# Queueing weight pieces behind the first tile's activation split in a two-layer decoder trunk

## The chip, the core and the metric

The kernel runs on one core of a Trainium2 chip. The metric is the device time of one execution in microseconds (us), launch to end; the median of the runs is what is compared. The engines are named as the profile names them: PE is TensorE, PEld its weight loads, DVE is VectorE, ACT is ScalarE, POOL is GpSimd, SP is the engine that issues the transfers.

## The reference

Two layers over 256 tokens of width 1024, all in float32. Every sub-layer is wrapped in two RMS norms, and the six of them follow one another: FFN, attention with short convolution, FFN, FFN, RWKV-7 mixing, FFN.

```python
def macaron_half_ffn(x, pre_g, post_g, w_gate, w_up, w_down):
    h = rmsnorm(x, pre_g)
    h = (jax.nn.silu(h @ w_gate) * (h @ w_up)) @ w_down
    return x + 0.5 * rmsnorm(h, post_g)

for i in range(DEPTH):
    x = macaron_half_ffn(x, *p["ffn1"])
    x = x + rmsnorm(p["mixer"](rmsnorm(x, pre_g), *p["mix"]), post_g)
    x = macaron_half_ffn(x, *p["ffn2"])
```

## The kernel before

**Tiles and parts.** The 256 tokens are two tiles of 128 rows, m=0 and m=1, kept in x0 and x1. The six sub-layers are six parts, so there are five places where a new part begins after another has ended. This text calls them start 1 (attention, near 190 to 203 us), start 2 (second FFN, near 337 to 352), start 3 (third FFN, near 527 to 541), start 4 (RWKV mixing, near 717 to 745) and start 5 (last FFN, near 954 to 968).

**Products in three passes.** A float32 product is made of three matmuls: each operand is split into a high part `hi`, rounded to the matmul type, and the rest `lo`; mm3 (lines 282 to 284) adds hi·hi, hi·lo and lo·hi. So each weight and each activation has to be split before TensorE can take it. For a weight piece of 128x1024, split_u and split_free issue one ACT copy (L241, `hi`) and then the subtraction (L246, `lo`), on DVE as one instruction, or on POOL as two halves of 128x512. Every `share`-th piece goes to POOL; `nlo` counts them. For activations `split` (L217 on ACT, L218 on DVE) does the same, from PSUM after a transpose.

**The end of a part.** out_proj multiplies with the last weight matrix. In its tail it first finishes tile 0 and then runs tile 1. As soon as tile 0's sums are there, post_norm(0) updates x0 (square sums on ACT at L297, L290; the power for 1/rms on POOL at L291; L353 and L356 on DVE), and `after(0)` calls the next part's start(0): pre_norm (L297, L314, L290, L291, L319), eight transposes (L326) and hT_split. The PE instructions of tile 1 from step PIN=15 on, the last three matmuls, stand behind those transposes. start(1) follows when tile 1 is done.

**What stands beside it.** While PE runs tile 1, the next part's first weights are loaded and split: in an FFN eight pieces for 512 columns, four of the gate matrix and four of the up matrix. This text counts them as piece 1, 2 and so on, in the order in which split_u is called. There are 18 buffers `u`, two a piece, and out_proj's tail holds most of them until tile 1 has used its weights.

**The order.** Instructions are put in order on each engine by a planner that runs a model of the chip while the program is built and takes, among those ready, the one that was written first. `issue_after(i)` adds one rule: an instruction on the engine of `i` comes behind `i`. pre_norm(0) sets `held` to three instructions, the last square sum (ACT), the last product with the gain (DVE, L314) and the power (POOL), and `free` to 4. split_u counts `free` down; the first four pieces are not held, all later ones stand behind `held`, each engine behind its own.

**In the RWKV part** l1_start takes the place of norm_in's start: it calls pre_norm and so sets `held` and `free` too, but transposes and copies by its own lines (L902 to L905). Its first pieces are one of w_r, two of mixed activations (L246 `u<-xn`), and a second one of w_r.

Of the kernel before, what the change touches and what calls it, by code (L numbers as in the profile page):

```python
# [8 lines left out]
F32 = mybir.dt.float32  # L9
F32R = mybir.dt.float32r  # L10
AF = mybir.ActivationFunctionType
ALU = mybir.AluOpType
# [17 lines left out]
class Trunk:  # L30
# [161 lines left out]
    def norm_in(self, gname):  # L192

        hilo = []

        def start(m, first=False):
            if m < 0:
                hilo.extend([(self.gain_cols if first else self.gain)(gname), *self.hl_tiles()])
                return
            g, *hl = hilo  # L200
            if g.shape[1] == KD:
                self.hT_split(self.pre_norm(m), hl, m, g)
            else:
                self.hT_split(self.pre_norm(m, g), hl, m)
        return hilo, start

    def gain(self, name):
# [6 lines left out]


    def split(self, src, hi, lo):
        self.nc.scalar.activation(hi, src, AF.Copy)  # L217
        return self.nc.vector.tensor_sub(lo, src, hi.bitcast(F32))  # L218

    def split_u(self, src):  # L220

# [6 lines left out]
    def split_free(self, src):  # L228
        n = src.shape[1]
        hi, lo = (self.u(F32R)[:, :n * src.shape[2]].rearrange("p (a b) -> p a b", a=n) for _ in range(2))  # L230
        self.nlo += 1
        if n == 1 and src.shape[2] == 512:

            if self.nlo % 3 == 0:
                self.nc.vector.tensor_copy(hi, src)
                self.nc.gpsimd.tensor_sub(lo, src, hi.bitcast(F32))
            else:
                self.split(src, hi, lo)
            return hi, lo
        pool = self.share and self.nlo % self.share == 0  # L240
        self.nc.scalar.activation(hi, src, AF.Copy)  # L241
        ax = 1 if n > 1 else 2
        m = src.shape[ax] // (2 if pool else 1)
        for i in range(0, src.shape[ax], m):
            c = (slice(None),) * ax + (slice(i, i + m),)
            (self.nc.gpsimd if pool else self.nc.vector).tensor_sub(lo[c], src[c], hi[c].bitcast(F32))  # L246
        return hi, lo
# [59 lines left out]
    def pre_norm(self, m, g=None):  # L307
        nc = self.nc
        xn, xg = self.xn(), self.x[m] if g is None else self.xn()
        ss = []  # L310
        for sl in self.HALF:
            self.tail_of["sq"] = self.sum_in(ss, xn[:, sl], self.x[m][:, sl], 1.0 / 32, EPS).ins
            if g is not None:
                self.tail_of["xg"] = nc.vector.tensor_tensor(xg[:, sl], self.x[m][:, sl], g[:, sl], op=ALU.mult).ins  # L314
        r = self.rstd(ss)
        if m == 0 and g is not None:
            self.held, self.free = list(self.tail_of.values()), 4
        for sl in self.HALF:
            nc.vector.tensor_scalar(xn[:, sl], xg[:, sl], r, None, op0=ALU.mult)  # L319
        return xn  # L320

    def transposed(self, src, n):
# [7 lines left out]
    def hT_split(self, xn, t, m, g=None):  # L330
        for h in range(2):
            pt = self.transposed(xn[:, h * 512:(h + 1) * 512], 4)
            hi, lo = (t[h][:, :, i, m * P:(m + 1) * P] for i in range(2))
            if g is None:
                self.split(pt, hi, lo)
                continue
            for i in range(4):
                k = h * 4 + i
                self.nc.scalar.activation(hi[:, i], pt[:, i, :], AF.Copy, scale=g[:, k:k + 1])
                self.nc.vector.scalar_tensor_tensor(lo[:, i], pt[:, i, :], g[:, k:k + 1], hi[:, i].bitcast(F32),  # L340
                                                    op0=ALU.mult, op1=ALU.subtract)

    def post_norm(self, m, g, half):

        nc = self.nc
        c = 0.5 if half else 1.0
        t, sq, ss = self.xn(), self.xn(), []

        def take(b):
            sl = self.HALF[len(ss)]  # L350
            self.sum_in(ss, sq[:, sl], b, 1.0 / (32 * c), EPS / (c * c))
            r = self.rstd(ss) if len(ss) == 2 else None
            nc.vector.tensor_mul(t[:, sl], b, g[:, sl])  # L353
            if r is not None:
                for sl in self.HALF:
                    nc.vector.scalar_tensor_tensor(self.x[m][:, sl], t[:, sl], r, self.x[m][:, sl],  # L356
                                                   op0=ALU.mult, op1=ALU.add)
        return take


    def out_proj(self, w, a, order, split, gname, half, after, by_k=False):
        ws = {}
        gpost = self.gain(gname)
# [14 lines left out]
        for i in range(split):  # L378
            for m in range(2):
                for hh in range(2):  # L380
                    step(i, m, hh)
            yield
        tail = range(split, len(order))
        take = self.post_norm(0, gpost, half)
        steps = [(i, hh) for hh in range(2) for i in tail]
# [1149 lines left out]
```

## Time and profile before

| | us |
|---|---|
| median of 3 runs | 1160.28 (1158.94 to 1164.31) |
| profiled execution | 1160.69 |
| its span in the trace | 1159.0 |
| PE busy in the span | 1093.6 |
| DVE busy | 701.2 |
| ACT busy | 601.0 |
| POOL busy | 429.6 |

The rows come from the one profiled execution. A row of the timeline gives the start in us, the length in us, the engine, the source line, the operation and its tiles, the shapes and a count where like instructions follow one another; in brackets stands the idle time before it and what released it. A row of the window view gives the window, its length, the busy time with the number of instructions, the granted TensorE clock as a share of full speed, and what the transfers did.

### The profile page before, as it was taken

What the parts mean: (1) busy time and instruction counts of PE and PEld (TensorE: products, weight loads), DVE (VectorE), ACT (ScalarE), POOL (GpSimd) and SP (SyncE); (2) the same over time, 40 slices, a digit from 0 to 9 for tenths busy, and PEclk for the clock granted to TensorE, in tenths of its full rate; (3) what the DMA queues carried; (4) which work ended last, traced back from release to release, by engine and by line L of the source; (5) the groups of instructions that cost most, each with busy time, mean ns of one, the idle gap of its engine ahead of it and who ended that gap; (6) DMA issues with size and microseconds to landing.
All of it is one profiled execution on the core that took longest, in us unless ns stands there. A gap on an engine that the chain in (4) does not pass through costs nothing.

```text
span 1159.0 us, 16840 instructions
## 1 busy us (share of the span) xinstructions
PE 1093.6 (94%) x6429; PEld 921.9 (80%) x6429; DVE 701.2 (61%) x1177; ACT 601.0 (52%) x1130; POOL 429.6 (37%) x390
## 2 busy tenths in 40 slices
PE   7999998998989999999999999997789789999997
PEld 5888887997967888887888888786447777888886
DVE  6655526656767655426655543889894797655531
ACT  7655545245645555435655542557554355655541
POOL 3523233232544333333532332334463553433331
PEclk9999999989999999999999999999996899999999
DMA  9765563442445765655566553442212144755530
GB/s 331 252 216 180 184 207 89 148 146 73 163 164 168 231 207 171 205 182 180 164 201 200 184 184 126 145 147 74 92 54 92 57 150 160 244 192 188 176 109 36
DMA packets 130749, 187.46 MB, mean 162 GB/s; under 512 B 6871, under 2 KB 101087, under 8 KB 130670
## 3 DMA queue, kind: packets, MB, share of 16 engines
q1 hardware_dynamic: 130670, 186.41, 48.7%
q8 instruction: 50, 0.82, 0.3%
q14 instruction: 29, 0.24, 0.1%
HBM read 185.34 MB, written 1.05 MB: 161 GB/s over the span
## 4 chain that ended last, share of the span: by engine, by line
PE 76%; DVE 15%; issue 4%; ACT 3%; POOL 1%; DMA 0%; SPq 0%; DVEq 0%; POOLq 0%; ACTq 0%
PE mm L429 10%; PE fl L429 10%; PE fl L284 7%; PE fl L282 6%; PE fl L283 6%; PE fl L430 5%; PE mm L430 5%; PE mm L282 5%; PE mm L284 5%; PE mm L283 5%; DVE u L246 3%; PE tr L326 2%; PE fl L433 1%; PE mm L433 1%; DVE xn L1220 1%
## 5 line engine op out<-in xcount | busy, mean ns | idle before, releaser
L246 POOL TENSOR_TENSOR u<-raw,u 128x512 fp32r<-128x512 f32 x222 | 321.7, 1471 | 496.1 <-ACT u L241 490.4
L241 ACT ACTIVATE u<-raw 128x1024 fp32r<-128x1024 f32 x312 | 327.5, 1058 | 276.7 <-PE mm L283 78.5
L246 DVE TENSOR_TENSOR u<-raw,u 128x1024 fp32r<-128x1024 f32 x201 | 272.7, 1362 | 210.5 <-ACT u L241 210.2
L429 PE MATMUL mm<-b,u 128*128 128x512 f32 x504 | 181.3, 398 | 0.0
L429 PE MATMUL fl<-b,u 128*128 128x512 f32 x504 | 180.6, 397 | 0.0
L430 PE MATMUL fl<-b,u 128*128 128x256 f32 x504 | 141.5, 281 | 0.0
L430 PE MATMUL mm<-b,u 128*128 128x256 f32 x504 | 141.4, 281 | 0.0
L284 PE MATMUL fl<-u,b 128*128 128x512 f32 (+1 forms) x304 | 118.4, 390 | 3.5 <-DVE b L218 3.0
L282 PE MATMUL fl<-u,b 128*128 128x512 f32 (+1 forms) x304 | 118.7, 393 | 2.6 <-DVE u L800 1.3
L283 PE MATMUL fl<-u,b 128*128 128x512 f32 (+1 forms) x304 | 118.4, 389 | 1.5 <-DVE u L246 1.5
L282 PE MATMUL mm<-u,b 128*128 128x512 f32 (+1 forms) x296 | 114.7, 389 | 0.0
L283 PE MATMUL mm<-u,b 128*128 128x512 f32 (+1 forms) x296 | 113.0, 383 | 0.0
L284 PE MATMUL mm<-u,b 128*128 128x512 f32 (+1 forms) x296 | 112.5, 382 | 0.0
L429 PEld LDWEIGHTS mm<-b,u 128*128 128x128 f32 x504 | 94.8, 188 | 19.7
L429 PEld LDWEIGHTS fl<-b,u 128*128 128x128 f32 x504 | 94.9, 188 | 19.5
L430 PEld LDWEIGHTS mm<-b,u 128*128 128x128 f32 x504 | 95.2, 189 | 3.3
L430 PEld LDWEIGHTS fl<-b,u 128*128 128x128 f32 x504 | 95.2, 189 | 3.1
L284 PEld LDWEIGHTS fl<-u,b 128*128 128x128 f32 x304 | 57.8, 190 | 16.9 <-DVE b L218 4.3
L282 PEld LDWEIGHTS fl<-u,b 128*128 128x128 f32 x304 | 58.0, 191 | 15.1 <-ACT b L217 2.0
L283 PEld LDWEIGHTS fl<-u,b 128*128 128x128 f32 x304 | 58.0, 191 | 12.9 <-DVE u L246 1.7
L282 PEld LDWEIGHTS mm<-u,b 128*128 128x128 f32 (+1 forms) x296 | 55.8, 189 | 11.8 <-issue 0.7
L283 PEld LDWEIGHTS mm<-u,b 128*128 128x128 f32 (+1 forms) x296 | 55.9, 190 | 10.6
(313 smaller groups left out, 1830.0 us busy)
## 6 DMA issues: line engine op xcount, KB each, us to landing
raw<-in_l_ffn_w_up_dram SPq DMA_DIRECT2D x44, 1024.0 KB, 7.3
raw<-in_l_ffn_w_down_dram SPq DMA_DIRECT2D x44, 1024.0 KB, 5.1
raw<-in_l_ffn_w_gate_dram SPq DMA_DIRECT2D x42, 1024.0 KB, 5.3
raw<-in_l_w_in_dram SPq DMA_DIRECT2D x9, 1024.0 KB, 5.2
raw<-in_l_w_v_dram SPq DMA_DIRECT2D x6, 1024.0 KB
raw<-in_l_w_out_dram SPq DMA_DIRECT2D x4, 1024.0 KB
raw<-in_l_w_r_dram SPq DMA_DIRECT2D x4, 1024.0 KB, 5.6
raw<-in_l_w_k_dram SPq DMA_DIRECT2D x4, 1024.0 KB, 5.2
```

The costliest lines, as they stand in the source:

```text
L241: self.nc.scalar.activation(hi, src, AF.Copy)
L246: (self.nc.gpsimd if pool else self.nc.vector).tensor_sub(lo[c], src[c], hi[c].bitcast(F32))
L282: mm(out, a[0], b[0], start=start, stop=False)
L283: mm(out, a[0], b[1], start=False, stop=False)
L284: mm(out, a[1], b[0], start=False, stop=stop)
L326: t = self.nc.tensor.transpose(pt[:, j * P:(j + 1) * P], src[:, j * P:(j + 1) * P], self.ident)
L429: mm(b2, w[k][0], x, start=k == 0, stop=False)
L430: mm(b2[:, 0], w[k][1], x[:, 0], start=False, stop=False)
L433: mm(b2, w[k][0], x, start=False, stop=True)
L1220: ins = [e.tensor_tensor(x, x, t, op=ALU.subtract) for e, x, _, _, t in act]
```

## The change

Three edits. pre_norm(0) no longer keeps the product with the gain in `held` but the second half of the scaling by 1/rms (L319), which comes later on DVE. norm_in's start(0), used by the FFN and attention parts, then replaces the first two entries of `held` by the last two instructions of hT_split: the ACT copy and the DVE subtraction of the second half of tile 0's transposed activations; the third entry, POOL's power, stays. And a piece that is free (`free` not yet below 0) is never given to POOL: its `lo` is one DVE instruction, whatever `nlo` says. `split` and hT_split return their instructions for this.

```diff
@@ norm_in
-                self.hT_split(self.pre_norm(m, g), hl, m)
+                hi, lo = self.hT_split(self.pre_norm(m, g), hl, m)
+                if m == 0:
+                    self.held[:2] = hi.ins, lo.ins
@@ split_free
-        pool = self.share and self.nlo % self.share == 0
+        pool = self.share and self.nlo % self.share == 0 and self.free < 0
@@ pre_norm
             if g is not None:
-                self.tail_of["xg"] = nc.vector.tensor_tensor(xg[:, sl], self.x[m][:, sl], g[:, sl], op=ALU.mult).ins
+                nc.vector.tensor_tensor(xg[:, sl], self.x[m][:, sl], g[:, sl], op=ALU.mult)
         r = self.rstd(ss)
+        for sl in self.HALF:
+            self.tail_of["xn"] = nc.vector.tensor_scalar(xn[:, sl], xg[:, sl], r, None, op0=ALU.mult).ins
         if m == 0 and g is not None:
-            self.held, self.free = list(self.tail_of.values()), 4
-        for sl in self.HALF:
-            nc.vector.tensor_scalar(xn[:, sl], xg[:, sl], r, None, op0=ALU.mult)
+            self.held, self.free = [self.tail_of[n] for n in ("sq", "xn", "pow")], 4
```

## Rows read from the trace of the kernel before

**Rows 1.** The page, busy time, share of the span and instructions of each engine.

```profile
PE 1093.6 (94%) x6429; PEld 921.9 (80%) x6429; DVE 701.2 (61%) x1177; ACT 601.0 (52%) x1130; POOL 429.6 (37%) x390
```

**Rows 2.** Timeline of PE at starts 1, 2, 3, 4 and 5.

```profile
198.60 1.09 PE L326 MATMUL tr<-ident,xn 128*128 128x128 f32 x8 [1.78 <-DVE xn L319]
...
202.46 0.50 PE L284 MATMUL fl<-u,b 128*128 128x512 f32 x1 [1.35 <-DVE b L218]
...
346.28 1.33 PE L326 MATMUL tr<-ident,xn 128*128 128x128 f32 x8 [4.06 <-DVE xn L319]
...
351.63 0.50 PE L284 MATMUL fl<-u,b 128*128 128x512 f32 x1 [1.09 <-DVE b L218]
...
536.66 0.66 PE L326 MATMUL tr<-ident,xn 128*128 128x128 f32 x4 [0.93 <-DVE xn L319]
538.07 0.66 PE L326 MATMUL tr<-ident,xn 128*128 128x128 f32 x4 [0.75 <-DVE xn L319]
...
540.90 0.50 PE L284 MATMUL fl<-u,b 128*128 128x512 f32 x1 [0.57 <-DVE b L218]
...
725.70 1.04 PE L326 MATMUL tr<-ident,xn 128*128 128x128 f32 x8
...
962.97 0.63 PE L326 MATMUL tr<-ident,xn 128*128 128x128 f32 x4 [1.29 <-DVE xn L319]
964.43 0.80 PE L326 MATMUL tr<-ident,xn 128*128 128x128 f32 x4 [0.84 <-DVE sse L300]
```

**Rows 3.** Windows of PE: busy time, count, granted clock, DMA share, GB/s.

```profile
346.00:351.00 5.00, 4.26 (x15) 0.66 0.20 49
...
535.00:538.00 3.00, 1.39 (x8) 1.00 0.42 110
...
541.00:551.00 10.00, 10.00 (x44) 1.00 0.93 314
...
965.00:968.00 3.00, 3.00 (x9) 0.50 0.49 134
```

**Rows 4.** Timeline of ACT at starts 1, 2 and 3.

```profile
193.29 0.30 ACT L290 ACTIVATE rstd<-ss,sse 128x1 f32<-128x1 f32 x1 [0.75 <-DVE sse L300]
...
336.99 0.28 ACT L290 ACTIVATE rstd<-ss,sse 128x1 f32<-128x1 f32 x1
...
344.03 2.93 ACT L241 ACTIVATE u<-raw 128x1024 fp32r<-128x1024 f32 x3
...
531.17 0.28 ACT L290 ACTIVATE rstd<-ss,sse 128x1 f32<-128x1 f32 x1
```

**Rows 5.** Timeline of POOL at starts 1, 2 and 3.

```profile
192.62 3.91 POOL L246 TENSOR_TENSOR u<-raw,u 128x512 fp32r<-128x512 f32 x2 [0.63 <-ACT u L241]
...
337.17 2.52 POOL L246 TENSOR_TENSOR u<-raw,u 128x512 fp32r<-128x512 f32 x2 [6.59 <-ACT u L241]
339.65 0.56 POOL L291 TENSOR_TENSOR rstd<-rstd,nhalf 128x1 f32<-128x1 f32 x1
...
531.34 4.24 POOL L246 TENSOR_TENSOR u<-raw,u 128x512 fp32r<-128x512 f32 x2 [4.13 <-ACT u L241]
```

**Rows 6.** Timeline of DVE at start 2, and one row of start 5.

```profile
340.25 1.41 DVE L356 SCALAR_TENSOR_TENSOR x<-xn,rstd,x 128x512 f32<-128x512 f32 x2 [3.38 <-POOL rstd L291]
341.58 1.29 DVE L314 TENSOR_TENSOR xn<-x,gain 128x512 f32<-128x512 f32 x2
...
345.65 0.88 DVE L319 TENSOR_SCALAR xn<-xn,rstd 128x512 f32<-128x512 f32 x2 [0.45 <-POOL rstd L291]
346.45 4.53 DVE L246 TENSOR_TENSOR u<-raw,u 128x1024 fp32r<-128x1024 f32 x2
350.90 1.27 DVE L218 TENSOR_TENSOR b<-tr,b 128x512 fp32r<-128x512 f32 x2
...
957.17 2.38 DVE L314 TENSOR_TENSOR xn<-x,gain 128x512 f32<-128x512 f32 x2
```

**Rows 7.** Line 246 on DVE: length of one in ns, shortest, median, longest; span of starts.

```profile
L246 DVE TENSOR_TENSOR u<-raw,u x201: 1207/1225/2358, 21.5 to 1126.5; 128x1024 fp32r<-128x1024 f32 x101
```

More of the change, by code (lines that the diff above doesn't have):

```diff
@@ L216, in split @@
     def split(self, src, hi, lo):
-        self.nc.scalar.activation(hi, src, AF.Copy)
-        return self.nc.vector.tensor_sub(lo, src, hi.bitcast(F32))
+        i = self.nc.scalar.activation(hi, src, AF.Copy)
+        return i, self.nc.vector.tensor_sub(lo, src, hi.bitcast(F32))
     def split_u(self, src):
@@ L334, in hT_split @@
             if g is None:
-                self.split(pt, hi, lo)
+                last = self.split(pt, hi, lo)
                 continue
@@ L341, in hT_split @@
                                                     op0=ALU.mult, op1=ALU.subtract)
+        return last if g is None else None
     def post_norm(self, m, g, half):
```

## The prediction

> **What bounds the kernel now.** The page's first part comes first: PE is busy 94% of the span, DVE and ACT little over half of it [rows 1]. A gain must therefore come out of the 65 us in which PE stands still, or out of stretches in which its clock is low. So the second view is PE's timeline, read only for rows with a bracket, in the stretches where one part ends and the next begins. At four of the five starts PE stands twice [rows 2]: before the transposes of tile 0 (released by L319 on DVE, the scaling by 1/rms, or by L300, a small DVE step behind it), and before the first L284, the first matmul that needs the `lo` of the transposed activations (released by L218 on DVE). Start 1 loses 1.78 + 1.35 = 3.13 us, start 2 4.06 + 1.09 = 5.15, start 3 0.93 + 0.75 + 0.57 = 2.25, start 5 1.29 + 0.84 = 2.13: 12.66 us together. Start 4 shows no bracket, so nothing can be won there on PE at once.
>
> The third view is the windows with the granted clock [rows 3]. Behind the stand of 4.06 us PE runs at 0.66 on average over 5 us, and behind the two stands of start 5 at 0.50, the lower level of 1.2 GHz, for 3 us; behind start 3's stands it keeps 1.00. At full clock a matmul of 512 columns follows the last after 10.00 us / 44 = 0.227 us. At start 5 nine are counted in the 3 us, where full speed needs some 2.0; with the slow transposes ahead of them I put the loss at 1.5 to 1.9 us. At start 2 15 instructions stand in the slow window; seven matmuls at double distance cost 7 x 0.227 = 1.6 us. The most that can be had is then 12.66 + 1.6 + 1.9 = 16.2 us.
>
> Last, ACT, POOL and DVE are read backwards from each stand to see what was late. At start 3 ACT has the sum ready at 531.17 + 0.28 = 531.45 [rows 4], but POOL is 4.24 us in a weight piece from 531.34 to 535.58 [rows 5], and the power, for which L319 waits, comes behind it. At start 1 the sum is ready at 193.59 and POOL is in a piece until 196.53; at start 2 at 337.27, and the power begins at 339.65 behind a piece of 2.52 us [rows 4, 5]. These are pieces 4, 4 and 4 of the new part: free ones, which the old hold lets by. Then at start 2 two pieces take DVE 4.53 us, from 346.45, directly ahead of L218 at 350.90 [rows 6]: held pieces, but held only behind L314.
>
> **Part one: free pieces leave POOL.** By the counting of `nlo`, and by the POOL rows at each start, nine pieces move: pieces 2 and 4 at start 1, 1 and 4 at starts 2, 3 and 4, piece 3 at start 5. Removed: 18 POOL halves, 1.26 us each undisturbed [rows 5]; added: nine DVE instructions at 1.21 to 2.36 us, median 1.23 [rows 7]. I take the median, since the long ones are those beside POOL work, which is what goes. Powers no longer wait: 196.53 - 193.59 = 2.9 us at start 1, about 2.3 at start 2, 4.1 at start 3, none at start 5. At start 5 the gain is on DVE: both L314 take 2.38 us beside a POOL piece and 1.29 where POOL is idle [rows 6], and the L356 pair ahead of them is lengthened alike, so some 2 us. What it costs: at most two pieces a start on DVE, 1.23 each, ready before the power is; POOL's wait was longer than the piece. At start 2 piece 4 can be ready at 337.1 and L356 at 337.9, so it pushes L356 by 0.4 at most.
>
> That a lengthening of DVE comes with POOL at work is what the two L314 rows show. The Trainium skill (SBUF — State Buffer, Who interferes with whom) says that a DVE instruction with two SBUF inputs and a GpSimd one that reads SBUF exclude each other for a whole instruction; by that rule, an estimate, nine pieces of two halves would give DVE back up to 18 x 1.26 = 23 us, of which only what lies on the chains above counts. The trace agrees in direction: 2.38 against 1.29 us.
>
> **Part two: the hold moves.** Pieces 5 and on now stand behind the second ACT copy and the second DVE subtraction of tile 0's split. Removed from in front of them: at start 2 4.53 us of DVE, and ACT's piece ahead of the second sum; at starts 3 and 5 one or two pieces each between the two halves of L218. At start 1 piece 5 stands there. What waits instead: each piece 5 to 8, its buffers, the transfers of the next raw weights that SP issues when a raw tile is done, and the up matmuls. Cover: behind the first L284 the gate product of tile 0 alone is 24 matmuls, 24 x 0.227 = 5.4 us, and four pieces cost ACT 2.93 / 3 = 0.98 each [rows 4], DVE 1.23 [rows 7], POOL 2.5 to 4.2 for its one [rows 5]. The second L218 ends 1.27 / 2 = 0.6 us behind the first [rows 6], so the first up piece is there 0.6 + 0.98 + 1.23 = 2.8 us after the first L284, POOL's, if it is the third, at 0.6 + 3 x 0.98 + 4.2 = 7.7 at worst, and the up product needs them at 5.4, 6.8, 8.2 and 9.5. So I cost the delay at nothing; without that cover it costs about 2.5 us a start. SP's transfers come as early as before: the pieces begin later relative to the norm, but the norm ends sooner.
>
> **Chain of start 2 with both edits.** Power at 337.3, L356 at 337.9 to 338.3 (1.41 us for the pair), L314 1.29 us, sum and power 1.0 to 1.2 us, L319 at 342.0: transposes at 342.5 or so. PE is free at 346.28 - 4.06 = 342.2. So of 4.06 about 0.3 to 0.8 stays; L218 no longer has the two pieces in front, which takes the 1.09; a stand under 1 us, like start 3's, leaves the clock at 1.00. I take 5.2 of at most 6.8. **Start 1:** the power is early enough that L319 is done before PE is free at 196.8, so 1.78 goes; of the 1.35 some stays, since splits by `split` (not held) also stand in front of L218: 2.3 of 3.13. **Start 3:** 2.0 of 2.25. **Start 5:** DVE's 2 us cover the first stand, 1.29, and with it I take half of the clock's 1.9; the second, 0.84, I leave, since piece 3 may take 1.2 of DVE: 2.2 of 4.0. **Start 4:** two more pieces on DVE, between -2.4 (both hidden, POOL's share of DVE time freed) and +2.5 (two medians in line); the first is split while DVE is idle and the second replaces a POOL piece, so 0. Sum: 5.2 + 2.3 + 2.0 + 2.2 = 11.7 us. Bounds: 16.2 + 2.4 = 18.6 at best; with the half of each start and +2.5 at start 4, 3.4 at worst of this case.
>
> **The rivals.** *A, only the POOL edit tells.* If what the planner put between the halves stays (free pieces and unheld splits fill the same places), the second stands remain: 1.8 + 2.3 + 1.0 + 1.3 = 6.4 us gained. For it: start 1 has unheld work; against: start 2's two pieces are held ones. *B, the up weights become the wait.* If DVE and ACT take tile 1's norm first (L356, L314, L319: 1.41 + 1.29 + 0.88 = 3.6 us [rows 6]), pieces 5 to 8 come 2.5 to 3.6 us later and PE waits that long at starts 2, 3 and 5, 7.5 to 10.8 us: net 0.9 to 4.2 gained, against it the 5.4 us of cover. *C, slower: DVE becomes the engine at the starts.* Its place is from L356 to L218. If all nine pieces stand in line there, they cost 9 x 1.23 to 9 x 2.36 = 11 to 21 us against the 6.4 that POOL's power gives: 5 to 15 us slower, 1170 in the middle. It decides where DVE's norm work (3.6 us) and its pieces exceed PE's remaining tile-1 matmuls: at start 2 those end 4.3 us after L356 can begin (337.9 to 342.2), so one piece tells there; at starts 1 and 3 the sum for L319's power is ready 3.2 and 4.3 us ahead of their end (193.59 to 196.82, 531.45 to 535.73), room for two. The Trainium skill (Perfetto Trace Analysis, Optimizing Scalar/DVE Operations) holds that offloading to GPSIMD may make sense where DVE is saturated, which speaks against taking pieces off POOL; DVE at 61% of the span [rows 1] and idle 3.38 us ahead of L356 [rows 6] shows that it isn't, here. *D, the change doesn't do what it says:* at start 4 it doesn't (no split in the hold); elsewhere the planner's model could already place the pieces late, and the time stays within 2 us of 1160.
>
> **How the numbers follow.** The profiled execution took 1160.69 us, 0.4 over the median of the runs: 1160.69 - 11.7 = 1149.0, which I give without taking off the 0.4. Chances: forecast (gain 8 to 18) 0.66; A 1154.3, 0.14; B 1156.5 to 1160, 0.08; C 0.06; D 0.06. Range: 1143.5 (nearly all of the bound) to 1156.5 (A with a loss at start 4). Differences under 0.5%, 5.8 us, can hardly be told from none. Faster by more: the forecast and most of A, 0.77; within: 0.17; slower: 0.06.
>
> **What would show it.** Right: POOL 390 - 18 = 372 instructions and DVE 1177 + 9 = 1186; no POOL L246 between the two powers of a start; no L246 on DVE between L319 and the second L218 unless of pieces 1 to 4; brackets before L326 of under 1 us at each start; a clock of 1.00 behind start 2. Wrong: PE brackets on `u` L246 or L241 some 5 us behind the first L284 (B), or L319 released by DVE's own queue rather than by POOL, with L246 in front (C). What would upset all of it: the planner orders anew, and the attention and RWKV parts between may come out differently by a few us either way.

## The result, and the profile after

The changed kernel took 1151.08 us (median of 4 runs, 1149.36 to 1152.56) against 1162.3 for the kernel before; the ratio is 0.9884, 95% interval 0.9843 to 0.9925. Two later measurements of the same program gave 0.992 (0.988 to 0.996) and 0.9895 (0.9863 to 0.9928). One execution of the third run below, of 1346.6 us at a granted clock of 0.75, is left out of its ratio. The profiled execution took 1152.56 us with a span of 1150.8, 8.2 under the span before. In the changed file the lines have moved by two or three: L328 are the transposes, L284 to L286 the three matmuls, L219 and L220 the activation split, L243 and L248 the weight pieces, L292 and L293 the sum and the power, L359 the update of x, L316 the product with the gain; L319 is still the scaling. In the runs below the numbers move by a few more; the operation and its tiles tell which step a row is.

The page's first part shows the pieces moved: POOL has 18 instructions fewer, DVE 9 more [rows 1].

```profile
PE 1092.3 (95%) x6429; PEld 918.5 (80%) x6429; DVE 701.9 (61%) x1186; ACT 600.1 (52%) x1130; POOL 406.9 (35%) x372
```

PE's timeline at the five starts: the transposes of tile 0, the first matmul that needs the `lo` of its activations, and the transposes of tile 1.

```profile
196.75 1.03 PE L328 MATMUL tr<-ident,xn 128*128 128x128 f32 x8
199.90 0.50 PE L286 MATMUL fl<-u,b 128*128 128x512 f32 x1 [0.71 <-DVE b L220]
208.89 1.07 PE L328 MATMUL tr<-ident,xn 128*128 128x128 f32 x8 [0.89 <-DVE xn L319]
...
338.56 1.06 PE L328 MATMUL tr<-ident,xn 128*128 128x128 f32 x8 [0.17 <-DVE xn L319]
340.62 0.47 PE L286 MATMUL fl<-u,b 128*128 128x512 f32 x1
352.78 1.06 PE L328 MATMUL tr<-ident,xn 128*128 128x128 f32 x8 [1.39 <-DVE xn L319]
...
526.64 1.03 PE L328 MATMUL tr<-ident,xn 128*128 128x128 f32 x8
528.67 0.47 PE L286 MATMUL fl<-u,b 128*128 128x512 f32 x1
540.84 1.07 PE L328 MATMUL tr<-ident,xn 128*128 128x128 f32 x8 [1.40 <-DVE xn L319]
...
952.65 1.06 PE L328 MATMUL tr<-ident,xn 128*128 128x128 f32 x8 [0.18 <-DVE xn L319]
954.71 0.48 PE L286 MATMUL fl<-u,b 128*128 128x512 f32 x1
968.69 1.29 PE L328 MATMUL tr<-ident,xn 128*128 128x128 f32 x8 [3.26 <-DVE xn L319]
```

In the kernel before no bracket stood before tile 1's transposes. Starts 2 and 5:

```profile
361.73 1.04 PE L326 MATMUL tr<-ident,xn 128*128 128x128 f32 x8
...
978.12 1.03 PE L326 MATMUL tr<-ident,xn 128*128 128x128 f32 x8
```

At tile 0 little is left of the stands of [rows 2]: 0.71, 0.17, nothing and 0.18 us. But four new ones stand before tile 1's transposes: 0.89, 1.39, 1.40 and 3.26. Set side by side, the same points of both traces tell what each was worth; "PE free" is the start of the transposes less the bracket.

| point | before | after | earlier by |
|---|---|---|---|
| start 1, PE free for tile 0 | 196.82 | 196.75 | 0.1 |
| first matmul with `lo` | 202.46 | 199.90 | 2.6 |
| first matmul behind tile 1's transposes | 211.75 | 210.58 | 1.2 |
| start 2, PE free | 342.22 | 338.39 | 3.8 |
| first with `lo` | 351.63 | 340.62 | 11.0 |
| behind tile 1 | 363.01 | 354.09 | 8.9 |
| start 3, PE free | 535.73 | 526.64 | 9.1 |
| first with `lo` | 540.90 | 528.67 | 12.2 |
| behind tile 1 | 552.29 | 542.15 | 10.1 |
| start 4, transposes | 725.70 | 717.17 | 8.5 |
| start 5, PE free | 961.68 | 952.47 | 9.2 |
| first with `lo` | 968.01 | 954.71 | 13.3 |
| behind tile 1 | 979.40 | 970.01 | 9.4 |
| end | 1159.0 | 1150.8 | 8.2 |

From "PE free" to the first matmul with `lo`, tile 0 gains 2.5 + 7.2 + 3.1 + 4.1 = 16.9 us; from there to the point behind tile 1's transposes 1.4 + 2.1 + 2.1 + 3.9 = 9.5 us are given back. At starts 2, 3 and 5 both sums hold some work that only changed sides: before, seven matmuls ran between the transposes and the first with `lo`, after, five. Two matmuls at 0.227 us are 0.45 a start, some 1.4 us in all. Without them tile 0 gains 2.5 + 6.7 + 2.7 + 3.6 = 15.5 us and tile 1 loses 1.4 + 1.6 + 1.6 + 3.5 = 8.1, of which 6.9 are its four stands. Behind two of the stands, at starts 3 and 5, a further 1.6 and 1.2 go to the clock, as the windows behind starts 2, 3 and 5 show:

```profile
352.00:357.00 5.00, 3.98 (x23) 1.00 0.80 288
541.00:546.00 5.00, 4.75 (x20) 0.67 0.61 223
968.00:973.00 5.00, 4.28 (x17) 0.66 0.05 15
```

The attention part between starts 1 and 2 gave another 2.7 us, of which more in the last section. Within it PE now waits twice for a weight piece, some 30 and 36 us behind start 1's tile 1; before, only 0.18 us stood in that stretch:

```profile
240.78 0.39 PE L286 MATMUL fl<-b,u 128*128 128x256 f32 x1 [0.73 <-DVE u L248]
...
246.78 0.38 PE L285 MATMUL mm<-u,b 64*128 64x256 f32 x1 [0.94 <-DVE u L220]
```

Why is tile 1 late? DVE and POOL at start 2, from the split of tile 0 to the scaling of tile 1:

```profile
339.85 1.29 DVE L220 TENSOR_TENSOR b<-tr,b 128x512 fp32r<-128x512 f32 x2 [1.05 <-ACT b L219]
341.28 1.23 DVE L248 TENSOR_TENSOR u<-raw,u 128x1024 fp32r<-128x1024 f32 x1
...
343.03 1.22 DVE L248 TENSOR_TENSOR u<-raw,u 128x1024 fp32r<-128x1024 f32 x1
344.69 3.48 DVE L359 SCALAR_TENSOR_TENSOR x<-xn,rstd,x 128x512 f32<-128x512 f32 x2 [0.44 <-POOL rstd L293]
...
348.69 1.21 DVE L248 TENSOR_TENSOR u<-raw,u 128x1024 fp32r<-128x1024 f32 x1
...
350.49 1.21 DVE L248 TENSOR_TENSOR u<-raw,u 128x1024 fp32r<-128x1024 f32 x1
352.14 0.88 DVE L319 TENSOR_SCALAR xn<-xn,rstd 128x512 f32<-128x512 f32 x2 [0.44 <-POOL rstd L293]
```

```profile
343.04 1.62 POOL L293 TENSOR_TENSOR rstd<-rstd,nhalf 128x1 f32<-128x1 f32 x1 [5.15 <-ACT rstd L292]
344.62 2.99 POOL L248 TENSOR_TENSOR u<-raw,u 128x512 fp32r<-128x512 f32 x2
351.09 1.02 POOL L293 TENSOR_TENSOR rstd<-rstd,nhalf 128x1 f32<-128x1 f32 x1 [3.48 <-ACT rstd L292]
```

The hold does what it says: no piece stands ahead of L220. But pieces 5 to 9 have not gone away. They now stand beside the norm of tile 1: DVE's pieces between its steps, and POOL's piece 7 over the update of x, which takes 3.48 us for the pair where it took 1.41 [rows 6]. At start 5 POOL costs twice. ACT has the sum ready at 957.05, POOL has just begun piece 6, and the power waits until 960.46; the update then meets POOL's next piece:

```profile
956.75 0.30 ACT L292 ACTIVATE rstd<-ss,sse 128x1 f32<-128x1 f32 x1
```

```profile
956.95 3.55 POOL L248 TENSOR_TENSOR u<-raw,u 128x512 fp32r<-128x512 f32 x2 [4.97 <-ACT u L243]
960.46 1.53 POOL L293 TENSOR_TENSOR rstd<-rstd,nhalf 128x1 f32<-128x1 f32 x1
961.96 2.98 POOL L248 TENSOR_TENSOR u<-raw,u 128x512 fp32r<-128x512 f32 x2
```

```profile
962.02 3.47 DVE L359 SCALAR_TENSOR_TENSOR x<-xn,rstd,x 128x512 f32<-128x512 f32 x2 [0.44 <-POOL rstd L293]
```

### The profile page after: what moved, and what is told of

It reads as the page before. It is cut to its first block, busy times and chain, and to the rows that moved or that the text cites. A ratio compares the mean times of both kernels' runs of the same rounds, so it can differ in the third digit from the quotient of the medians.

```text
span 1150.8 us, 16819 instructions
## 1 busy us (share of the span) xinstructions
PE 1092.3 (95%) x6429; PEld 918.5 (80%) x6429; DVE 701.9 (61%) x1186; ACT 600.1 (52%) x1130; POOL 406.9 (35%) x372
## 4 chain that ended last, share of the span: by engine, by line
PE 73%; DVE 13%; issue 5%; ACT 4%; POOL 2%; DMA 1%; SPq 0%; DVEq 0%; POOLq 0%; ACTq 0%
PE fl L432 10%; PE mm L432 10%; PE fl L284 6%; PE fl L286 6%; PE fl L285 6%; PE mm L433 5%; PE fl L433 5%; PE mm L284 5%; PE mm L285 5%; PE mm L286 5%; DVE u L248 2%; PE tr L328 2%; ACT u L243 2%; PE mm L436 1%; PE fl L436 1%
## 5 line engine op out<-in xcount | busy, mean ns | idle before, releaser
L243 ACT ACTIVATE u<-raw 128x1024 fp32r<-128x1024 f32 x312 | 327.5, 1059 | 277.8 <-PE fl L435 78.5
L248 POOL TENSOR_TENSOR u<-raw,u 128x512 fp32r<-128x512 f32 x204 | 295.0, 1468 | 472.4 <-ACT u L243 468.3
L248 DVE TENSOR_TENSOR u<-raw,u 128x1024 fp32r<-128x1024 f32 x210 | 280.1, 1340 | 216.7 <-ACT u L243 216.1
L284 PE MATMUL fl<-u,b 128*128 128x512 f32 (+1 forms) x304 | 119.1, 394 | 1.7 <-ACT b L219 1.1
L286 PE MATMUL fl<-u,b 128*128 128x512 f32 (+1 forms) x304 | 119.3, 394 | 1.1 <-DVE b L220 0.7
L284 PE MATMUL mm<-u,b 128*128 128x512 f32 (+1 forms) x296 | 114.3, 388 | 0.0
L286 PE MATMUL mm<-u,b 128*128 128x512 f32 (+1 forms) x296 | 112.0, 380 | 0.0
L293 POOL TENSOR_TENSOR rstd<-rstd,nhalf 128x1 f32<-128x1 f32 x24 | 21.2, 882 | 144.6 <-ACT rstd L292 144.6
L284 PEld LDWEIGHTS fl<-u,b 128*128 128x128 f32 x304 | 58.2, 192 | 14.5 <-ACT b L219 2.3
L286 PEld LDWEIGHTS fl<-u,b 128*128 128x128 f32 x304 | 58.2, 191 | 14.3 <-DVE b L220 1.7
L285 PEld LDWEIGHTS mm<-u,b 128*128 128x128 f32 (+1 forms) x296 | 55.8, 189 | 12.2 <-DVE u L220 1.1
```

The source lines that it names most:

```text
L284: mm(out, a[0], b[0], start=start, stop=False)
L285: mm(out, a[0], b[1], start=False, stop=False)
L286: mm(out, a[1], b[0], start=False, stop=stop)
L293: self.tail_of["pow"] = nc.gpsimd.tensor_tensor(r2, r, self.nhalf, op=ALU.pow).ins
```

## The experiments

**Each edit alone.** The first run has only the rule that free pieces stay off POOL, in the kernel before:

```diff
-        pool = self.share and self.nlo % self.share == 0
+        pool = self.share and self.nlo % self.share == 0 and self.free < 0
```

> The first edit alone: free pieces never go to POOL, the hold stays behind the product with the gain. Theory (both edits are needed at tile 0, and the hold is what pushes pieces 5 to 9 into tile 1's norm): PE's first stand before tile 0's transposes shrinks at starts 1 to 3 (1.78, 4.06, 0.93 us before) to under 1, 2 and 0.5, the second stands before the first matmul that needs the low part (1.35, 1.09, 0.57) stay within 0.5 of that, and no stand of over 0.7 appears before tile 1's transposes; 1154 to 1157 us. Rival (the POOL edit is the whole of it): 1149 to 1152, with tile-1 stands as in the changed kernel (0.9, 1.4, 1.4, 3.3).

It took 1152.2 us, ratio 0.989 (0.985 to 0.993): the same as both edits together. PE's timeline at tile 0 of starts 1 and 2, tile 1 of start 3 and tile 0 of start 5:

```profile
200.83 0.50 PE L284 MATMUL fl<-u,b 128*128 128x512 f32 x1 [1.44 <-DVE b L218]
...
343.48 1.06 PE L326 MATMUL tr<-ident,xn 128*128 128x128 f32 x8 [1.26 <-DVE xn L319]
...
543.41 1.03 PE L326 MATMUL tr<-ident,xn 128*128 128x128 f32 x8
...
958.08 0.63 PE L326 MATMUL tr<-ident,xn 128*128 128x128 f32 x4 [2.12 <-DVE xn L319]
```

The first stands shrink at starts 1 to 3 as the theory says (1.78 to nothing, 4.06 to 1.26, 0.93 to nothing), and tile 1 has none. The second stands went further down than expected at starts 2 and 3 (0.29 and nothing), and the median was 2 us under the expected range. At start 5 the stands grow: 2.12 and 0.78 us for 1.29 and 0.84. The scaling there takes 2.90 us for the pair, beside POOL's next piece (956.38, 2.68 us), which the old hold lets by as soon as the power is done:

```profile
956.45 2.90 DVE L319 TENSOR_SCALAR xn<-xn,rstd 128x512 f32<-128x512 f32 x2 [0.76 <-POOL rstd L291]
```

The time fits the rival, the tile-1 stands don't: the two kernels reach the same time by different ways.

The second run has only the hold, with the POOL rule as before:

```diff
-        pool = self.share and self.nlo % self.share == 0 and self.free < 0
+        pool = self.share and self.nlo % self.share == 0
```

> The second edit alone: the hold moves behind the split of tile 0, free pieces go to POOL as before. Theory: the powers still wait for POOL pieces 4, so 1 to 2 us stay before tile 0's transposes at starts 1 to 3, while the second stands go (under 0.4 each); tile 1's stands at starts 2, 3 and 5 appear as in the changed kernel, over 1 us each; 1154 to 1160 us. Rival (the hold is the whole of it): 1149 to 1152.

It took as long as the kernel before: ratio 1.0014 (0.998 to 1.005). Its stands came as the theory had them: at tile 0 1.77, 2.40, none and 0.77 us before the transposes and 0.22 at most behind them; at tile 1 0.92, 1.39, 1.40 and 3.28. Tile 0 at start 2, then tile 1 at starts 2 and 5:

```profile
343.10 1.07 PE L328 MATMUL tr<-ident,xn 128*128 128x128 f32 x8 [2.40 <-DVE xn L319]
...
357.32 1.07 PE L328 MATMUL tr<-ident,xn 128*128 128x128 f32 x8 [1.39 <-DVE xn L319]
...
976.86 1.94 PE L328 MATMUL tr<-ident,xn 128*128 128x128 f32 x8 [3.28 <-DVE xn L319]
```

What it wins at tile 0 it pays at tile 1. Its median of 1164.8 us lies above the expected range, partly because the range left the second half of this sum out, partly because the kernel before took 1164.5 us beside it and not the 1160.3 on record.

**Is it POOL that delays tile 1?** The third run is the changed kernel, with pieces 5 to 9 of the attention and FFN parts kept off POOL as well; `quiet` is -5 there and 0 in the RWKV part:

```diff
-        pool = self.share and self.nlo % self.share == 0 and self.free < 0
+        pool = self.share and self.nlo % self.share == 0 and self.free < self.quiet
```

> The changed kernel, and at the starts of attention and FFN parts pieces 5 to 9 are kept off POOL too (all on DVE). Theory (tile 1's stands come from POOL pieces beside tile 1's norm: two-step x update 3.48 us beside POOL against 1.41, and at start 5 the power behind a piece): x update at 1.4 to 1.6 us at starts 2, 3 and 5, tile-1 stands from 1.39, 1.40 and 3.26 to under 0.5 each, 4 to 7 us less than the changed kernel, 1144 to 1147. Rival (tile 1's chain is as long as that anyway, PE only arrives sooner; pieces on DVE then lengthen it): stands of 1.4 to 3.3 stay or grow, 1150 to 1153.

It took 1142.6 us, ratio 0.9808 (0.977 to 0.984), and in a later measurement (below) 0.9818: better than both kernels. DVE's update of x at start 2, then PE: behind tile 1's transposes at start 1, at tile 0's transposes at start 2, and at tile 1's at starts 2, 3 and 5:

```profile
343.70 1.42 DVE L361 SCALAR_TENSOR_TENSOR x<-xn,rstd,x 128x512 f32<-128x512 f32 x2 [0.44 <-POOL rstd L294]
```

```profile
210.57 0.50 PE L285 MATMUL fl<-u,b 128*128 128x512 f32 x1 [1.70 <-ACT b L220]
...
337.57 1.07 PE L330 MATMUL tr<-ident,xn 128*128 128x128 f32 x8 [1.19 <-DVE xn L320]
...
350.86 1.06 PE L330 MATMUL tr<-ident,xn 128*128 128x128 f32 x8 [0.53 <-DVE xn L320]
...
538.02 1.06 PE L330 MATMUL tr<-ident,xn 128*128 128x128 f32 x8 [0.54 <-DVE xn L320]
...
961.05 1.07 PE L330 MATMUL tr<-ident,xn 128*128 128x128 f32 x8 [0.53 <-DVE xn L320]
```

1.39, 1.40 and 3.26 become 0.53, 0.54 and 0.53, PE comes to tile 0 no later than in the changed kernel, and DVE has more pieces, not fewer. At these three starts the rival, a chain that is as long as that anyway, falls. At start 1 nothing is won: the 0.89 goes, but PE then waits 1.70 for ACT behind the transposes, and the matmul there begins at 210.57, in the changed kernel at 210.58. Start 2 gets a stand of 1.19 at tile 0, where PE now arrives 2.0 us sooner.

The time was a little under the range expected, and not all of it comes from the stands. Between the two profiles lie 8.9 us. On the points of the table above, starts 2, 3 and 5 give 3.6 of them, the stretches from start 3 to start 4 and from start 5 to the end 2.9 (the clock behind tile 1 is 1.00 here, 0.67 and 0.66 in the changed kernel), and the attention part 2.0: its two waits for weight pieces, 0.73 and 0.94, are gone, at the same clock of 0.98 between 215 and 320 us.

The fourth run asks whether piece 9 needs to be there at all: pieces 5 to 8 off POOL, and those from 9 on behind tile 1's split and power.

```diff
-            for i in self.held if self.free < 0 else ():
+            for i in () if self.free >= 0 else self.later if self.later and self.free < -4 else self.held:
```

> As the run before it, but only pieces 5 to 8 are kept off POOL, and pieces 9 and later stand behind tile 1's split and power. Theory: pieces 5 to 8 are all that tile 0 and 1 need, piece 9 stood beside tile 1's norm for nothing: tile-1 stands under 0.3, 1143 to 1147 us. Rival (the later hold makes the following weights late): PE stands on u some 11 us behind tile 1's transposes, 1 to 3 us a start, 1148 to 1155.

1143.5 us, ratio 0.9825 (0.979 to 0.986). The brackets before tile 1's transposes are gone at starts 2, 3 and 5, and no stand on `u` takes their place, but the time can't be told from that of the third run: what was left to win there was 0.53 + 0.54 + 0.53 = 1.6 us.

**Does the hold do anything?** Pieces 1 to 9 off POOL, and the hold of the kernel before:

```diff
-        pool = self.share and self.nlo % self.share == 0
+        pool = self.share and self.nlo % self.share == 0 and self.free < self.quiet
```

> Pieces 1 to 9 kept off POOL at the attention and FFN starts, with the hold of the kernel before (behind the product with the gain). Theory (the new hold is worth something only when POOL is out of tile 1's way): pieces 5 to 9 on DVE come ahead of tile 0's split again, second stands of 1 to 2 us at starts 1, 2 and 5, and a first one there, no stand before tile 1's transposes over 0.6; 1147 to 1152 us, 5 to 9 more than with the new hold. Rival (the hold is worth nothing, keeping POOL quiet is all): 1141 to 1145.

1152.0 us, ratio 0.9919 (0.9887 to 0.995). So with POOL out of the way the hold is worth 0.9919 against 0.9808 and 0.9818, about 1%; with POOL in it, nothing (0.989 against 0.9884). Stands came back at tile 0, one a start and not the two expected: 1.43 and 1.17 before the first matmul with `lo` at starts 1 and 3, 2.17 and 2.06 before the transposes at starts 2 and 5. Tile 1 has none, as expected. DVE at start 2 takes three pieces in a row between the scaling and the split; then PE before the transposes:

```profile
338.94 0.87 DVE L322 TENSOR_SCALAR xn<-xn,rstd 128x512 f32<-128x512 f32 x2
339.73 3.49 DVE L248 TENSOR_TENSOR u<-raw,u 128x1024 fp32r<-128x1024 f32 x3
343.13 1.28 DVE L220 TENSOR_TENSOR b<-tr,b 128x512 fp32r<-128x512 f32 x2
```

```profile
339.56 1.93 PE L329 MATMUL tr<-ident,xn 128*128 128x128 f32 x8 [2.17 <-DVE xn L322]
```

The three pieces stand behind the scaling, so the 2.17 us before the transposes are not theirs. The scaling itself follows the power, which ends at 338.78, by 0.16 us. Before the first matmul with `lo` PE has no bracket here: behind the stand its clock is 0.66 (338 to 343), and it is still busy when the split is done.

**Reads or any work of POOL?** The changed kernel, with zeros written by POOL in place of its subtractions for pieces 5 to 9:

```diff
+            if pool and self.ffn_start and -6 < self.free < 0:
+                self.nc.gpsimd.memset(lo[c].bitcast(F32), 0.0)
+                continue
```

> The changed kernel, but where one of pieces 5 to 9 goes to POOL at an attention or FFN start, POOL writes zeros instead of subtracting, so the low part of those weights is left out. POOL then writes to SBUF at the same place in its queue and reads nothing, and DVE has no more work than in the changed kernel. Theory (DVE is slowed by POOL's reads): tile 1's x update takes 1.4 to 1.6 us at starts 2, 3 and 5, not 3.5, and the tile-1 stands go under 0.6; 1143 to 1147. Rival (any POOL work beside it, or DVE's own order, makes it long): x update stays over 2.5.

One execution took 1145.06 us; the tile-1 stands at starts 2, 3 and 5 are gone and the updates take 1.41 to 1.42. But the fill waits for no ACT copy, so the planner put it 7.6 us ahead of the update at start 2, beside the scaling of tile 0, and 6.5 ahead at start 3, just behind that scaling; the test is narrower than it was meant. Only at start 5 does one lie beside the update. POOL, then DVE, at starts 2 and 5:

```profile
336.74 0.98 POOL L250 MEMSET u<- 128x512 f32 x2
...
956.70 0.99 POOL L250 MEMSET u<- 128x512 f32 x2
```

```profile
336.83 1.57 DVE L323 TENSOR_SCALAR xn<-xn,rstd 128x512 f32<-128x512 f32 x2 [0.21 <-POOL rstd L297]
...
956.79 1.42 DVE L364 SCALAR_TENSOR_TENSOR x<-xn,rstd,x 128x512 f32<-128x512 f32 x2 [0.44 <-POOL rstd L297]
```

Beside a POOL that only writes, the update, which reads two tiles, keeps its 1.42 us; the scaling, which reads one, goes from 0.88 to 1.57. The Trainium skill (SBUF — State Buffer, Who interferes with whom) says both: two SBUF inputs on DVE meet GpSimd's reads but not its writes, and `tensor_scalar` may use both of DVE's ports and then meets either. The trace agrees, by one overlap for the first and two for the second (1.58 at start 5).

**The two kernels side by side.** The changed kernel and the third run were measured again.

> The changed kernel once more, beside the two others of this call. 1149 to 1153 us, tile-1 stands of 0.9, 1.4, 1.4 and 3.3 us at starts 1, 2, 3 and 5.

> The kernel that keeps pieces 1 to 9 off POOL and has the new hold, once more, beside the changed kernel on the same chip. Theory (POOL out of the way and the hold together): a ratio to the kernel before of 0.979 to 0.985, 7 to 11 us under the changed kernel. Rival (the difference between the calls was the chip's): a ratio within 0.004 of the changed kernel's.

> The changed kernel beside it: a ratio to the kernel before of 0.988 to 0.993; tile-1 stands of 0.9, 1.4, 1.4 and 3.3 us at starts 1, 2, 3 and 5 as in its other profiles.

The third run came to 0.9818 (0.9789 to 0.9847) beside 0.9895 (0.9863 to 0.9928) for the changed kernel measured with it: 0.8% under it, with no overlap. The changed kernel's stands at tile 1 were the same in all three of its profiles (1.39 to 1.41 at starts 2 and 3, 3.24 to 3.26 at start 5).

## Why the prediction was right, and where it was not

**The number.** 1149.0 was forecast, 1151.08 measured; the forecast gain of 11.7 us compares with 11.2 between medians and 8.1 between the two profiled executions. That it came so near is luck. The 11.7 us were all tile 0's; tile 0 gave 3.8 more than that, tile 1 and the clock behind it took 10.9 that the sum doesn't have, and the parts between the starts, which it put at nothing, gave 3.6, much of it perhaps the clock (last section). What is left, 8.2 us between the spans, is 3.5 under the forecast; the runs' medians lie further apart than the two profiles.

**Tile 0 was sized too low.** 11.7 of at most 16.2 us was taken; 15.5 came, counted without the two matmuls that changed sides. Start 2 gave 6.7 for 5.2, start 3 2.7 for 2.0, start 5 3.6 for 2.2, start 1 2.5 for 2.3. The chain of start 2 was worked out to transposes at 342.5 with PE free at 342.2, a stand of 0.3; 0.17 was measured. What I took off for free pieces and unheld splits ahead of the `lo` step was not needed, save at start 1 (0.71). The clock behind start 2 stayed at full, as said. At start 5 the reason was wrong: I let DVE's 2 us of part one cover the first stand, but the two stands, 2.13 us together, grew to 2.90 with the POOL edit alone and fell to 0.77 with the hold alone. There it is the hold, which keeps POOL's piece off the scaling, that takes most of them.

**"So I cost the delay at nothing" is the step that failed.** For the pieces that the hold puts back I asked who waits for them, found the up product, and its cover of 5.4 us did hold: no PE bracket on a weight stands between the first `lo` matmul and tile 1's transposes at starts 1, 2, 3 and 5. I didn't ask what they would then stand beside. Tile 1's norm follows on the same DVE and POOL, and its scaling has PE waiting: 8.1 us, and 2.8 of clock. Rival B named that norm, but let it push the pieces, not the pieces push it; its sum, 7.5 to 10.8 us lost at starts 2, 3 and 5, is not far from the 6.7 of those three, 9.5 with the clock, but for the wrong wait. The signs given for B, brackets on `u` some 5 us behind the first L284, would have missed it. Waits on `u` did come, 0.73 and 0.94 us in the attention part, but the POOL edit alone has both (0.72 and 0.94), so they are not the hold's own.

**The rivals.** A, the POOL edit alone, was given 1154.3 us and 0.14; alone it took 1152.2, as much as the whole change. So what A says of the time is true, though its mechanism isn't what the trace shows: the second stands did go, and were paid for. C didn't come: at starts 1, 2, 3 and 5 of the changed kernel the scaling begins 0.03 to 0.04 us behind the power, so it doesn't wait for DVE's queue. With the old hold and POOL quiet it follows the power by 0.16 us at start 2, and that is all of C that is seen there. But the pieces moved to DVE have a price that I left out: the power takes 2.21 us at starts 1 and 3, where two of them lie beside it, and 0.56 at start 2, where none does. It cost no stand, since the scaling was done 0.9 us before PE came. D was wrong at four starts and right at start 4, where nothing stands; start 4 was put at 0, and from there to start 5 PE came 0.7 us earlier.

**What was shown, and what argued.** That POOL's pieces beside tile 1 make its stands at starts 2, 3 and 5 is shown by the third run. At start 1 its scaling begins at 208.26, before the change at 208.48: there the chain is as late as it was and PE comes sooner. That at start 5 the power behind piece 6 has its share, 3.4 of the wait, is read from the rows; no run took the one without the other.

## What to carry to other kernels

When background work is held back from one critical chain, look for the next chain on the same engines before counting the gain: here the hold alone was worth nothing, POOL's quiet alone 1%, and the two together, with POOL quiet past the second chain too, 1.8 to 1.9%. An engine that does one small step of a critical chain in order, as POOL does the power here, should be kept free of long background pieces for as long as that chain runs, even if another engine then does more.

## What the runs showed of the hardware

The same program, with the same stands at starts 1 to 3, had spans of 1147.9 and 1157.7 us in two executions. The windows over the attention part of both, the shorter first:

```profile
215.00:320.00 105.00, 99.41 (x756) 0.98 0.36 120
```

```profile
215.00:320.00 105.00, 101.24 (x720) 0.89 0.31 101
```

At a granted clock of 0.89 against 0.98 the part got 36 matmuls less done in the same 105 us, and start 2 came 6.8 us later. So most of the 2.7 us that the attention part seemed to give (a clock of 0.95 in this window in the profiled execution before, 0.98 in that after) may be the clock of those two executions. PE's stands in the part add up to 6.2 us before and 5.4 after, which leaves some 0.8 to the new order; no run separates the two, and it stays open.

A stand of the same length doesn't always bring the clock down: behind the 1.40 us at start 3 it was 0.67 in the first profile of the changed kernel (above) and 1.00 in the two others, behind 1.41 and 1.39 us. The second:

```profile
541.00:546.00 5.00, 4.72 (x26) 1.00 0.65 237
```
